# Memory tokens by rows, key/value weights by whole blocks, and two weight blocks at once where an operand's last rows come late

## The chip, the cores and the metric

The kernel runs on one core of one Trainium2 chip. The metric is the time of one execution in device microseconds (us). An execution has one long program for the engines: TensorE (PE, matmuls; PEld is its loading of weights), VectorE (DVE), ScalarE (ACT), GpSimd (POOL) and SyncE (SP), which issues nearly all DMAs.

## What is computed

One layer of a causal decoder, for 1024 tokens of width 1024 in float32. Cut to what matters here:

```python
h = rms_norm(x, norm_mix_pre)
z_pool, z_q, z_rwkv, z_gate = split(h @ w_in)
y_pool = pool_branch(z_pool) @ w_proj_pool       # windows 2, 4, 8, 16 over the tokens
kv     = rms_norm(mem, mem_norm) @ w_mem_kv      # 256 memory tokens, 4 heads of 128
y_mem  = attention(z_q, kv) @ w_proj_mem
y_rwkv = rwkv7(z_rwkv) @ w_proj_rwkv             # 16 heads of 64
gates  = sigmoid(z_gate + gate_b)
merged = gates[0] * y_pool + gates[1] * y_rwkv + gates[2] * y_mem
x = x + rms_norm(merged @ w_o, norm_mix_post)
f = conv_ffn(rms_norm(x, norm_ffn_pre))
x = x + rms_norm(f, norm_ffn_post)
```

## The kernel before

Activations lie transposed: 8 chunks (KC) of 128 channels on the partitions, tokens along the row, in two halves of 512. Each float32 product is made of three matmuls (`mm3`, L164): an operand is split into a high part, cast to the matmul's type (names ending in h or hi), and the rest (l or lo); the three are hi x hi (L167), hi weight x low operand (L168), low weight x hi operand (L169). So each weight chunk has to be split too. `load_w` (L143) loads one block of weights, 1024 rows by 128 columns, in pieces of two chunks (128 KB, tile `wraw`, three buffers for each class c, 0 or 1); `split_w` casts a piece on ACT (`whi`, L128) and subtracts on POOL (`wlo`, L131), or on DVE while `lo_on_dve` is set. `whi` and `wlo` have four buffers a class, one whole block. The classes alternate unless one is asked for, and each has its two PSUM tiles `psg`.

A scheduler sets the order of every engine's instructions ahead of time, from a cost model and priorities; at run time each engine goes through its own row in order and waits on semaphores. `later(a, b)` only sets the order: a is not put ahead of b. Blocks of `w_in` (the products for gates, queries and pooling) are placed into the row of PE as fill between dependent work. They go to DRAM (`d_zg`, `d_zq`, `d_zp`) and are read back later; in the profile they are `psg<-hh` and `psg<-hl`.

The stages that the change touches, in order of time:

- Memory tokens (L744 to L757): one DMA brings `memT` (1 MB, 8 chunks of 128x256) into `mraw`. ACT squares each chunk (`msq`), PE adds the squares over the channels with a matrix of ones (`pmm`, L749), ACT makes 1/rms (`mrs`), DVE scales `mraw` and splits it into `mh`, `ml`.
- Keys and values (L759 on): 8 blocks of `w_kv`, with 256 tokens on the free side; blocks 0 to 3 give K, 4 to 7 give V, which PE also transposes (`pvt`).
- Pooling's sums (`pool_sums`, L779): four loads `tz` of 512 KB from `d_zp`, some six DVE instructions each.
- Attention, four heads, with pooling's products and fill blocks in between; then the projections of attention (`pm`) and pooling (`g`, L886 to L892), each times its gate.
- Merge (`merge`, L911): `yh`, `yl` are the RWKV output, loaded as `yr` and split chunk by chunk (L121, L122; yh0 to yh7). For each half n and each block j: product with `w_prwkv`, times gate, plus `pm`, split into `mgh[j]` and `mgl[n][j]`. `yh`, `yl` of the last chunks lie in memory that pooling's `g` and its operands used before.
- Output product (`wo_gemm`, L1077): 8 blocks of `w_o` on `mgh`, `mgl`, for each half. The blocks of half 1 are started as soon as the merge of half 1 is through.

Of the kernel before, what the change touches and what calls it, by code (L numbers as in the profile page):

```python
# [9 lines left out]
F32 = mybir.dt.float32  # L10
FR = mybir.dt.float32r
AF = mybir.ActivationFunctionType
ALU = mybir.AluOpType
# [4 lines left out]
P = 128  # L18
T = 1024
D = 1024  # L20
KC = D // P
# [23 lines left out]
def trunk_kernel(ctx: ExitStack, tc: tile.TileContext, xT, memT, pvec, w_in, w_kv, w_upd, w_upg,  # L45
                 w_pool, w_ppool, w_pmem, w_prwkv, w_o, w_fup, w_fdn, out):
    nc = tc.nc
    V, A, G, PE, SP = nc.vector, nc.scalar, nc.gpsimd, nc.tensor, nc.sync

    const = ctx.enter_context(tc.tile_pool(name="const", bufs=1))  # L50
    wp = ctx.enter_context(tc.tile_pool(name="wp", bufs=1))
    psg = ctx.enter_context(tc.tile_pool(name="psg", bufs=2, space=PSUM))
# [5 lines left out]
    def dtile(shape, name):  # L58
        return dram.tile(shape, F32, name=name, tag=name)

    d_zp = dtile([4, P, T], "d_zp")
# [12 lines left out]
    def col(name, i):  # L74
        o, w = PV[name]
        return pv[:, o + i:o + i + 1]

    ones = const.tile([P, P], F32, name="ones")
# [16 lines left out]
    for lo in (0, 64):  # L95
        s = slice(lo, lo + 64)
# [3 lines left out]
    for lo in (0, 64):  # L100
        s = slice(lo, lo + 64)
# [18 lines left out]
    def split(src, hi, lo, lo_eng=None):  # L120
        A.copy(hi, src)  # L121
        return (lo_eng or V).tensor_tensor(lo, src, hi.bitcast(F32), op=ALU.subtract)  # L122
# [3 lines left out]
    def split_w(src, hi, lo):  # L126
        if hi_on_act[0]:
            A.copy(hi, src)  # L128
        else:
            G.tensor_scalar(hi, src, 1.0, 0.0, op0=ALU.mult, op1=ALU.add)  # L130
        (V if lo_on_dve[0] else G).tensor_tensor(lo, src, hi.bitcast(F32), op=ALU.subtract)  # L131

    def split_ps(ps, hi, lo):
        split(ps, hi, lo, V)
# [8 lines left out]
    def load_w(ap, nk, kp=2, c=None):  # L143
        if c is None:
            cls[0] ^= 1
            c = cls[0]
        ps = Ws()
        ps.c = c
        for k0 in range(0, nk, kp):
            load_more(ps, ap, k0, min(kp, nk - k0), kp)  # L150
        return ps

    def load_more(ps, ap, k0, n, kp):
        raw = wp.tile([P, kp, P], F32, name="wraw", tag=f"wraw{ps.c}", bufs=3)
        hi = wp.tile([P, kp, P], FR, name="whi", tag=f"whi{ps.c}", bufs=4)
        lo = wp.tile([P, kp, P], FR, name="wlo", tag=f"wlo{ps.c}", bufs=4)
        SP.dma_start(raw[:, :n], ap[:, k0:k0 + n])
        split_w(raw[:, :n], hi[:, :n], lo[:, :n])
        for j in range(n):
            ps.append((hi[:, j], lo[:, j]))  # L160

    last_mm = [None]

    def mm3(ps, w, x, start, stop):  # L164
        wh, wl = w
        xh, xl = x
        first = PE.matmul(ps, wh, xh, start=start, stop=False)  # L167
        PE.matmul(ps, wh, xl, start=False, stop=False)  # L168
        last_mm[0] = PE.matmul(ps, wl, xh, start=False, stop=stop).ins  # L169
        return first  # L170

    def gemm(ws, rhs, width=512, behind=None, ps=None, log=None):

        if ps is None:
            ps = psg.tile([P, 512], F32, name="psg", tag=f"g{getattr(ws, 'c', 0)}")[:, :width]
        n = len(ws)
        for k in range(n):
            m = mm3(ps, ws[k], rhs(k), k == 0, k == n - 1)
            if k == 0 and behind is not None:
                later(m, behind)  # L180
            if log is not None:
                log.append(last_mm[0])
        return ps
# [23 lines left out]
    def later(i, ins):  # L207

        tc.add_manual_dep(i.ins, ins.name, nosync, reason="order")
# [13 lines left out]
    for k in range(KC):  # L223
        tag = ("X01", "X11", "HV", "HV")[k // 2]
# [59 lines left out]

    def hrhs(t0):
        return lambda k: (hh[:, k, t0:t0 + 512], hl[:, k, t0:t0 + 512])

    def in_block(j, evac, c=0, log=None):
        ws = load_w(w_in[j], KC, c=c)
        for t0, _ in HALVES:  # L290
            evac(t0, gemm(ws, hrhs(t0), log=log))
# [448 lines left out]
    vh = kvp.tile([P, 4, 2, P], FR, name="vh")  # L740
    vl = kvp.tile([P, 4, 2, P], FR, name="vl")
    with tc.tile_pool(name="km", bufs=1) as km:
        mraw = km.tile([P, KC, 256], F32, name="mraw")
        SP.dma_start(mraw, memT.rearrange("(k p) t -> p k t", p=P))  # L744
        pmm = psk.tile([P, 512], F32, name="pmm", tag="k")
        for k in range(KC):
            sq = km.tile([P, 256], F32, name="msq", tag="msq", bufs=2)
            A.activation(sq, mraw[:, k], AF.Square)
            PE.matmul(pmm[:, :256], ones, sq, start=k == 0, stop=k == KC - 1)  # L749
        mrs = km.tile([P, 256], F32, name="mrs", tag="msq", bufs=2)  # L750
        rstd(mrs, pmm[:, :256], 0)
        mh = km.tile([P, KC, 256], FR, name="mh")
        ml = km.tile([P, KC, 256], FR, name="ml")
        for k in range(KC):
            V.scalar_tensor_tensor(mraw[:, k], mraw[:, k], col("mem_norm", k), mrs, op0=ALU.mult,
                                   op1=ALU.mult)
            split(mraw[:, k], mh[:, k], ml[:, k], V)  # L757
        lo_on_dve[0] = True
        for j in range(8):  # L759
            ws = load_w(w_kv[j], KC, c=0)  # L760
            ps = gemm(ws, lambda k: (mh[:, k], ml[:, k]), 256)
            if j < 4:
                split_ps(ps, kh[:, j], kl[:, j])
            else:
                vt = km.tile([P, 256], F32, name="vt", tag="msq", bufs=2)
                A.copy(vt, ps)
                pvt = psk.tile([P, 2, P], F32, name="pvt", tag="k")
                for m in range(2):
                    PE.transpose(pvt[:, m], vt[:, m * P:(m + 1) * P], ident)
                split(pvt, vh[:, j - 4], vl[:, j - 4], V)  # L770

        lo_on_dve[0] = False
# [6 lines left out]
    def pool_sums(gi):  # L779
        win = 2 << gi  # L780
        z = pb.tile([P, T], F32, name="tz", tag=f"p{gi}")
        SP.dma_start(z, d_zp[gi])
        two = [pb.tile([P, T], F32, name="ts2", tag=f"l{gi}"),
               pz.tile([P, T], F32, name="ts2", tag="ts") if gi else None]
        cur = z
        w = 1
        n = 0
        while w < win:
            nxt = two[n % 2]
            V.tensor_copy(nxt[:, 0:w], cur[:, 0:w])  # L790
            V.tensor_tensor(nxt[:, w:], cur[:, w:], cur[:, :T - w], op=ALU.add)
            cur = nxt
            w *= 2
            n += 1
        V.tensor_tensor(cur[:, 0:win], cur[:, 0:win], inv[:, 0:win], op=ALU.mult)
        V.tensor_scalar(cur[:, win:], cur[:, win:], 1.0 / win, None, op0=ALU.mult)
        V.tensor_tensor(z, cur, z, op=ALU.subtract)
        zs.append(z)
# [24 lines left out]
    for hd in range(4):  # L823
        for t0, _ in HALVES:
            s = slice(t0, t0 + 512)
# [6 lines left out]
            for u in range(2):  # L832
                ps = psg.tile([P, 2, 256], F32, name="psco", tag="g0")
# [41 lines left out]
    for j in range(8):  # L875
        ws = load_w(w_pmem[j], 4)
        for n, (t0, _) in enumerate(HALVES):
            s = slice(t0, t0 + 512)
            SP.dma_start(pm[j][n], d_zg[16 + j][:, s])
            act(pm[j][n], pm[j][n], AF.Sigmoid)  # L880
            ps = gemm(ws, lambda k: (oh[k][:, s], ol[k][:, s]))
            V.tensor_tensor(pm[j][n], pm[j][n], ps, op=ALU.mult)
    for j in range(8):
        ws = load_w(w_ppool[j], 4)
# [3 lines left out]
        for n, (t0, _) in enumerate(HALVES):  # L888
            s = slice(t0, t0 + 512)
            ps = gemm(ws, lambda k: (ph_[k][:, s], pl_[k][:, s]))  # L890
# [8 lines left out]
    yh, yl = [], []  # L899
# [7 lines left out]
    mgh = [at.tile([P, T], FR, name=f"mgh{k}", tag=f"m{k}") for k in range(KC)]  # L907

    mgl = [[], []]

    def merge(n, js):  # L911
        s = slice(n * 512, n * 512 + 512)
        for j in js:
            ws = load_w(w_prwkv[j], KC)
            gt = yp.tile([P, 512], F32, name="g1", tag="g1", bufs=4)
            SP.dma_start(gt, d_zg[8 + j][:, s])
            act(gt, gt, AF.Sigmoid)
            ps = gemm(ws, lambda k: (yh[k][:, s], yl[k][:, s]))
            V.tensor_tensor(gt, gt, ps, op=ALU.mult)
            V.tensor_tensor(gt, gt, pm[j][n], op=ALU.add)  # L920
            ml_ = pmp.tile([P, 512], FR, name=f"mgl{j}{n}", tag=f"n{2 * j + n}")
            mgl[n].append(ml_)
            split(gt, mgh[j][:, s], ml_, V)
# [148 lines left out]
        rstd(rs, ps, 0)  # L1072
        return rs

    os_, sss = [], []

    def wo_gemm(n, js):  # L1077
        s = slice(n * 512, n * 512 + 512)
        for j in js:
            if j == 0:  # L1080
                o = [(ow if n == 0 else ow1).tile([P, 2, 512], F32, name="o", tag=f"q{4 * n + a}") for a in range(4)]
                os_.append([o[k // 2][:, k % 2] for k in range(KC)])
                sss.append(ow.tile([P, 512], F32, name="ss", tag="ss", bufs=2))
            ws = load_w(w_o[j], KC)
            ps = gemm(ws, lambda k: (mgh[k][:, s], mgl[n][k]))
            V.tensor_copy(os_[n][j], ps)
            sumsq(sss[n], ps, j == 0, V)

# [470 lines left out]
```

## Time and profile before

| what | value |
|---|---|
| time, median of 3 runs | 2114.05 us (2111.07 to 2119.24) |
| profiled execution | 2115.82 us, its span 2114.1 us |
| granted clock of PE, mean | 0.991 |
| busy: PE, DVE, ACT, POOL | 2043.8, 1351.6, 1074.3, 810.1 us |
| DMA | 221.83 MB, mean 105 GB/s |

The profile is of one execution. In its lists an instruction is named by the line of the kernel, the engine, the operation and output<-inputs; `[2.4 <-ACT yh L121]` behind a row says that the engine stood idle for 2.4 us ahead of it and which instruction ended that. SPq is the queue in which SP issues DMAs; the DMA lists end with the median time from issue to landing. Ends of matmuls are modelled, so the text reads PE by the distances between starts: a matmul's row is longer than its distance to the next one.

### The profile page before, as it was taken

Reading aid. Unit: us, or ns where it says so; the run is one execution under the profiler, and the core shown is the slowest. Engines: PE = TensorE matmul, PEld = TensorE weight load, DVE = VectorE, ACT = ScalarE, POOL = GpSimd, SP = SyncE. Lnnn points to the kernel's source line nnn. Section 1 sums busy time; section 2 is a strip of 40 time slices with the busy share of each in tenths; the row PEclk is TensorE's granted clock in tenths of the full one; section 3 lists DMA queues with packets and bytes.
Section 4 is the critical chain, followed back from the end, with each engine's and each line's share of the span. In section 5 each row is a group of like instructions: output and inputs, shape, how many; then the busy total and the mean of one; then the engine's idle time right before and its main releaser. Section 6 shows DMA issues by size and latency. Waiting matters only on the chain.

```text
span 2114.1 us, 34140 instructions
## 1 busy us (share of the span) xinstructions
PE 2043.8 (97%) x12246; PEld 1565.2 (74%) x12246; DVE 1351.6 (64%) x2159; ACT 1074.3 (51%) x2252; POOL 810.1 (38%) x925
## 2 busy tenths in 40 slices
PE   8999999999999999999999999998999999999997
PEld 5777766776768666876777878776778877777886
DVE  6567437654657347733597442668867777776698
ACT  7584347623763367434467244545544444454644
POOL 5521112121122011212021255555678888842341
PEclk9999999999999999999999999999999999999999
DMA  4312111120212021213436343634222222159766
GB/s 153 127 40 78 64 61 58 61 81 22 85 63 90 27 88 43 85 54 115 153 103 221 111 138 102 210 110 152 90 95 75 75 80 80 66 163 280 163 181 155
DMA packets 179193, 221.83 MB, mean 105 GB/s; under 512 B 16720, under 2 KB 131536, under 8 KB 179024
## 3 DMA queue, kind: packets, MB, share of 16 engines
q1 hardware_dynamic: 166096, 204.44, 29.6%
q0 software_dynamic: 11856, 14.16, 4.1%
q8 instruction: 97, 1.59, 0.3%
q10 hardware_dynamic: 1072, 1.05, 0.1%
q14 instruction: 72, 0.59, 0.1%
HBM read 170.30 MB, written 49.28 MB: 104 GB/s over the span
## 4 chain that ended last, share of the span: by engine, by line
PE 44%; DVE 7%; DMA 6%; POOL 6%; ACT 5%; issue 4%; SPq 0%; POOLq 0%; ACTq 0%; DVEq 0%
PE psg L167 9%; PE psg L169 9%; PE psg L168 9%; POOL wt L999 3%; PE psd L168 2%; PE psd L169 2%; PE psd L167 2%; PE psf L169 2%; PE psf L168 2%; PE psf L167 2%; POOL wlo L131 2%; POOL sm L984 1%; DMA a<-in_w_fup 1%; DMA R<-d_f 1%; ACT d L1015 1%
## 5 line engine op out<-in xcount | busy, mean ns | idle before, releaser
L131 POOL TENSOR_TENSOR wlo<-wraw,whi 128x256 fp32r<-128x256 f32 x480 | 413.6, 870 | 987.5 <-ACT whi L128 827.6
L169 PE MATMUL psg<-hh,wlo 128*128 128x512 f32 x928 | 381.0, 411 | 7.4 <-POOL wlo L131 7.1
L167 PE MATMUL psg<-hh,whi 128*128 128x512 f32 x928 | 382.6, 412 | 0.0
L168 PE MATMUL psg<-hl,whi 128*128 128x512 f32 x928 | 377.8, 407 | 0.0
L128 ACT CAST whi<-wraw 128x256 fp32r<-128x256 f32 x496 | 193.7, 404 | 268.1 <-PE psg L168 153.0
L169 PEld LDWEIGHTS psg<-hh,wlo 128*128 128x128 f32 x928 | 174.8, 188 | 54.9 <-POOL wlo L131 14.2
L167 PEld LDWEIGHTS psg<-hh,whi 128*128 128x128 f32 x928 | 175.3, 189 | 41.7 <-issue 2.2
L168 PEld LDWEIGHTS psg<-hl,whi 128*128 128x128 f32 x928 | 175.4, 189 | 41.0 <-issue 2.2
L999 POOL TENSOR_TENSOR wt<-a,wt 128x256 fp32r<-128x256 f32 x136 | 134.3, 1016 | 28.6 <-ACT wt L998 28.6
L167 PE MATMUL psd<-f,u 128*128 128x512 f32 x292 | 115.1, 395 | 6.2 <-ACT f L1297 3.6
L168 PE MATMUL psd<-f,u 128*128 128x512 f32 x292 | 114.9, 394 | 0.9 <-DVE f L1301 0.9
L169 PE MATMUL psd<-f,u 128*128 128x512 f32 x292 | 114.2, 392 | 0.9 <-DVE u L1301 0.9
L999 POOL TENSOR_TENSOR wt<-sm,wt 128x256 fp32r<-128x256 f32 x102 | 106.9, 1068 | 15.7 <-ACT wt L998 15.7
L169 PE MATMUL psf<-h2h,wt 128*128 128x512 f32 x272 | 108.2, 398 | 0.2
L167 PE MATMUL psf<-h2h,wt 128*128 128x512 f32 x272 | 106.7, 392 | 1.3 <-ACT wt L998 1.3
L168 PE MATMUL psf<-h2l,wt 128*128 128x512 f32 x272 | 106.8, 393 | 0.0
L998 ACT CAST wt<-sm 128x256 fp32r<-128x256 f32 x102 | 37.9, 404 | 131.1 <-POOL sm L984 125.7
L1017 DVE SCALAR_TENSOR_TENSOR d<-z,pv,d 128x1023 f32<-128x1023 f32 x68 | 91.7, 1348 | 12.1 <-ACT d L1015 9.5
L169 PE MATMUL psf<-t,wt 128*128 128x512 f32 x204 | 81.2, 398 | 2.2 <-POOL wt L999 2.1
L168 PE MATMUL psf<-t,wt 128*128 128x512 f32 x204 | 80.3, 394 | 0.0
L167 PE MATMUL psf<-t,wt 128*128 128x512 f32 x204 | 80.3, 393 | 0.0
L674 DVE TENSOR_TENSOR HV<-ph,Hd 64x128 f32<-64x128 f32 x112 | 32.3, 288 | 71.5 <-PE ph L630 47.6
(420 smaller groups left out, 4736.6 us busy)
## 6 DMA issues: line engine op xcount, KB each, us to landing
wraw<-in_w_in SPq DMA_DIRECT2D x240, 128.0 KB, 2.4
a<-in_w_fup SPq DMA_DIRECT2D x128, 128.0 KB, 2.4
d_zg<-st SPq DMA_DIRECT2D x48, 256.0 KB, 2.6
wraw<-in_w_fup SPq DMA_DIRECT2D x80, 128.0 KB, 2.4
fw<-in_w_fdn SPq DMA_DIRECT2D x33, 256.0 KB, 4.8
fraw<-d_f SPq DMA_DIRECT2D x33, 256.0 KB, 5.4
wraw<-in_w_prwkv SPq DMA_DIRECT2D x64, 128.0 KB, 2.4
wraw<-in_w_o SPq DMA_DIRECT2D x64, 128.0 KB, 2.4
```

Of the source, the lines that this page charges most:

```text
L128: A.copy(hi, src)
L131: (V if lo_on_dve[0] else G).tensor_tensor(lo, src, hi.bitcast(F32), op=ALU.subtract)
L167: first = PE.matmul(ps, wh, xh, start=start, stop=False)
L168: PE.matmul(ps, wh, xl, start=False, stop=False)
L169: last_mm[0] = PE.matmul(ps, wl, xh, start=False, stop=stop).ins
L674: ready = V.tensor_tensor(HV[q, :, c + 1, e], ph[q], Hd[q], op=ALU.add).ins
L984: eng.tensor_tensor(out_[u], a[u], b[u], op=op)
L998: A.copy(w[0][:, us], src[u])
L999: last_low[0] = G.tensor_tensor(w[1][:, us], src[u], w[0][:, us].bitcast(F32), op=ALU.subtract).ins
L1015: A.activation(d, z, AF.Identity, scale=col("cw2", j), bias=col("cb", j))
L1017: V.scalar_tensor_tensor(d[:, n:], z[:, :T - n], col(cw, j), d[:, n:], op0=ALU.mult, op1=ALU.add)
```

## The change

- The memory tokens are loaded by eight DMAs of one chunk each (128 KB) into two tiles of four chunks with the tag `mraw`; the four `tz` loads are ordered behind the last `pmm` matmul.
- The weights of key/value blocks 2 to 7 are loaded by one DMA of 512 KB each into the same two buffers (`kvr`, tag `mraw`), once the tokens, or an earlier block, have been split out of them. The splits write the same `whi`, `wlo` buffers of class 0 as before.
- `two_gemms` makes two blocks' products at once: the first `late` chunks of the first block, then of the second, then the chunks left of the first and of the second. It is used for the first two blocks of merge, half 0 (late = 6), and of the output product, half 1 (late = 7).

```diff
+    def two_gemms(wss, rhs, late):
+
+        pss_ = [psg.tile([P, 512], F32, name="psg", tag=f"g{ws.c}") for ws in wss]
+        for ks in (range(late), range(late, KC)):
+            for ws, ps in zip(wss, pss_):
+                for k in ks:
+                    mm3(ps, ws[k], rhs(k), k == 0, k == KC - 1)
+        return pss_
...
-        mraw = km.tile([P, KC, 256], F32, name="mraw")
-        SP.dma_start(mraw, memT.rearrange("(k p) t -> p k t", p=P))
+        mraw = [km.tile([P, 4, 256], F32, name="mraw", tag="mraw", bufs=2) for _ in range(2)]
+        mraw = [mraw[k // 4][:, k % 4] for k in range(KC)]
+        for k in range(KC):
+            SP.dma_start(mraw[k], memT[k * P:(k + 1) * P])
...
-            PE.matmul(pmm[:, :256], ones, sq, start=k == 0, stop=k == KC - 1)
+            last_mm[0] = PE.matmul(pmm[:, :256], ones, sq, start=k == 0, stop=k == KC - 1).ins
+        mem_read = last_mm[0]
...
+        def kv_weights(j):
+            raw = km.tile([P, KC, P], F32, name="kvr", tag="mraw", bufs=2)
+            SP.dma_start(raw, w_kv[j])
+            ws = Ws()
+            ws.c = 0
+            for k in range(0, KC, 2):
+                hi, lo = (wp.tile([P, 2, P], FR, name=nm, tag=nm + "0", bufs=4) for nm in ("whi", "wlo"))
+                split_w(raw[:, k:k + 2], hi, lo)
+                ws.extend((hi[:, e], lo[:, e]) for e in range(2))
+            return ws
+
         for j in range(8):
-            ws = load_w(w_kv[j], KC, c=0)
+            ws = kv_weights(j) if j > 1 else load_w(w_kv[j], KC, c=0)
...
-        SP.dma_start(z, d_zp[gi])
+        later(SP.dma_start(z, d_zp[gi]), mem_read)
...
     def merge(n, js):
         s = slice(n * 512, n * 512 + 512)
+        rhs = lambda k: (yh[k][:, s], yl[k][:, s])
+        two = two_gemms([load_w(w_prwkv[j], KC) for j in js[:2]], rhs, 6) if n == 0 else []
         for j in js:
-            ws = load_w(w_prwkv[j], KC)
+            ws = None if two else load_w(w_prwkv[j], KC)
...
-            ps = gemm(ws, lambda k: (yh[k][:, s], yl[k][:, s]))
+            ps = two.pop(0) if two else gemm(ws, rhs)
...
-            ws = load_w(w_o[j], KC)
-            ps = gemm(ws, lambda k: (mgh[k][:, s], mgl[n][k]))
+            rhs = lambda k: (mgh[k][:, s], mgl[n][k])
+            if n == 1 and j == 0:
+                two.extend(two_gemms([load_w(w_o[e], KC) for e in range(2)], rhs, KC - 1))
+            ps = two.pop(0) if two else gemm(load_w(w_o[j], KC), rhs)
```

What this does to the order of instructions. On SP, from the memory tokens on, before:

```order
L744 DMA mraw<-in_memT 128x8x256
L782 DMA tz<-d_zp 128x1024 x4
L318 DMA d_zg<-st 128x512
L157 DMA wraw<-in_w_in 128x256 x4
L157 DMA wraw<-in_w_kv 128x256
L157 DMA wraw<-in_w_in 128x256
L157 DMA wraw<-in_w_kv 128x256 x2
L318 DMA d_zg<-st 128x512
L157 DMA wraw<-in_w_kv 128x256 x4
```

and now (`kvr` are the whole key/value blocks, `uraw` pooling's own weights):

```order
L755 DMA mraw<-in_memT 128x256 x8
L157 DMA wraw<-in_w_in 128x256 x3
L806 DMA tz<-d_zp 128x1024 x4
L774 DMA kvr<-in_w_kv 128x1024
L157 DMA wraw<-in_w_kv 128x256
L774 DMA kvr<-in_w_kv 128x1024
L346 DMA uraw<-in_w_pool 128x128 x2
L327 DMA d_zg<-st 128x512
L157 DMA wraw<-in_w_in 128x256
L346 DMA uraw<-in_w_pool 128x128
L327 DMA d_zg<-st 128x512
L346 DMA uraw<-in_w_pool 128x128
```

The eight rows come first, then three pieces of `w_in` that stood behind `tz`; the key/value loads are fewer, and pieces of `w_in` and stores of `d_zg` stand between them.

On PE, at the memory tokens, before (`pmm<-msq` are the sums of squares, `psg` the fill):

```order
L167 MATMUL psg_10834<-hh_142,whi_10817 128x512
L168 MATMUL psg_10834<-hl_143,whi_10817 128x512
L749 MATMUL pmm_9453<-msq_9454,ones_85 128x256
L749 MATMUL pmm_9453<-msq_9457,ones_85 128x256
L169 MATMUL psg_10834<-hh_142,wlo_10818 128x512
L749 MATMUL pmm_9453<-msq_9460,ones_85 128x256
L749 MATMUL pmm_9453<-msq_9463,ones_85 128x256
L167 MATMUL psg_10834<-hh_142,whi_10817 128x512
L749 MATMUL pmm_9453<-msq_9466,ones_85 128x256
L749 MATMUL pmm_9453<-msq_9469,ones_85 128x256
L168 MATMUL psg_10834<-hl_143,whi_10817 128x512
L749 MATMUL pmm_9453<-msq_9472,ones_85 128x256
```

and now:

```order
L168 MATMUL psg_10587<-hl_143,whi_10554 128x512
L169 MATMUL psg_10587<-hh_142,wlo_10555 128x512
L760 MATMUL pmm_9461<-msq_9462,ones_85 128x256
L760 MATMUL pmm_9461<-msq_9465,ones_85 128x256
L167 MATMUL psg_10587<-hh_142,whi_10554 128x512
L760 MATMUL pmm_9461<-msq_9468,ones_85 128x256
L760 MATMUL pmm_9461<-msq_9471,ones_85 128x256
L168 MATMUL psg_10587<-hl_143,whi_10554 128x512
L760 MATMUL pmm_9461<-msq_9474,ones_85 128x256
L760 MATMUL pmm_9461<-msq_9477,ones_85 128x256
L169 MATMUL psg_10587<-hh_142,wlo_10555 128x512
L760 MATMUL pmm_9461<-msq_9480,ones_85 128x256
```

The sums stand 11 rows, all of them fill matmuls, sooner in PE's row; as before, one fill matmul stands behind each second sum.

On PE, at the first block of merge, before (`psg_12130` is the first block's product, `psg_12187` the second's; yh6, yl6, yh7, yl7 are the last two chunks):

```order
L167 MATMUL psg_12130<-yh5_12075,whi_12116 128x512
L168 MATMUL psg_12130<-yl5_12076,whi_12116 128x512
L169 MATMUL psg_12130<-yh5_12075,wlo_12117 128x512
L167 MATMUL psg_12130<-yh6_12081,whi_12122 128x512
L168 MATMUL psg_12130<-yl6_12082,whi_12122 128x512
L169 MATMUL psg_12130<-yh6_12081,wlo_12123 128x512
L167 MATMUL psg_12130<-yh7_12087,whi_12122 128x512
L167 MATMUL psg_12187<-yh0_12045,whi_12161 128x512
L168 MATMUL psg_12130<-yl7_12088,whi_12122 128x512
```

and now, where the second block begins and where the first is taken up again (`psg_12123` the first block's, `psg_12124` the second's):

```order
L167 MATMUL psg_12123<-yh5_12047,whi_12088 128x512
L168 MATMUL psg_12123<-yl5_12048,whi_12088 128x512
L169 MATMUL psg_12123<-yh5_12047,wlo_12089 128x512
L167 MATMUL psg_12124<-yh0_12017,whi_12100 128x512
L168 MATMUL psg_12124<-yl0_12018,whi_12100 128x512
```

```order
L168 MATMUL psg_12124<-yl5_12048,whi_12112 128x512
L169 MATMUL psg_12124<-yh5_12047,wlo_12113 128x512
L167 MATMUL psg_12123<-yh6_12053,whi_12094 128x512
L168 MATMUL psg_12123<-yl6_12054,whi_12094 128x512
L169 MATMUL psg_12123<-yh6_12053,wlo_12095 128x512
L167 MATMUL psg_12123<-yh7_12059,whi_12094 128x512
L168 MATMUL psg_12123<-yl7_12060,whi_12094 128x512
```

Behind chunk 5 of the first block now stand chunks 0 to 5 of the second, 18 matmuls, and only then yh6. In the output product the same is done with 21 matmuls ahead of chunk 7.

More of the change, by code (lines that the diff above doesn't have):

```diff
@@ L747, in trunk_kernel @@
             sq = km.tile([P, 256], F32, name="msq", tag="msq", bufs=2)
-            A.activation(sq, mraw[:, k], AF.Square)
-            PE.matmul(pmm[:, :256], ones, sq, start=k == 0, stop=k == KC - 1)
+            A.activation(sq, mraw[k], AF.Square)
+            last_mm[0] = PE.matmul(pmm[:, :256], ones, sq, start=k == 0, stop=k == KC - 1).ins
+        mem_read = last_mm[0]
         mrs = km.tile([P, 256], F32, name="mrs", tag="msq", bufs=2)
@@ L754, in trunk_kernel @@
         for k in range(KC):
-            V.scalar_tensor_tensor(mraw[:, k], mraw[:, k], col("mem_norm", k), mrs, op0=ALU.mult,
+            V.scalar_tensor_tensor(mraw[k], mraw[k], col("mem_norm", k), mrs, op0=ALU.mult,
                                    op1=ALU.mult)
-            split(mraw[:, k], mh[:, k], ml[:, k], V)
+            split(mraw[k], mh[:, k], ml[:, k], V)
         lo_on_dve[0] = True
+        def kv_weights(j):
[8 more added lines that the diff above has]
+            return ws
         for j in range(8):
-            ws = load_w(w_kv[j], KC, c=0)
+            ws = kv_weights(j) if j > 1 else load_w(w_kv[j], KC, c=0)
             ps = gemm(ws, lambda k: (mh[:, k], ml[:, k]), 256)
@@ L1073, in norm @@
         return rs
-    os_, sss = [], []
+    os_, sss, two = [], [], []
     def wo_gemm(n, js):
```

## Prediction

> **What bounds the kernel now.** I read the profile's first part for the engine that carries the span, then the waits of TensorE (PE), then the stretches around the four edited places, then their rows in order of time.
>
> ```profile
> PE 2043.8 (97%) x12246; PEld 1565.2 (74%) x12246; DVE 1351.6 (64%) x2159; ACT 1074.3 (51%) x2252; POOL 810.1 (38%) x925
> ```
>
> PE is busy for 97% of the span, so a change that leaves PE's instructions as they are, as this one does, can only win what PE loses in waits or at a low clock. The list of PE's waits (in all, times, longest) has three at the edited places:
>
> ```profile
> PE psg L167 <- ACT yh L121: 2.4, 1, 2.4
> PE pmm L749 <- ACT msq L748: 2.3, 1, 2.3
> PE psg L167 <- ACT mgh L121: 1.8, 1, 1.8
> ```
>
> Each is one single wait. By stretch (PE, PEld, DVE, ACT, POOL busy; granted clock; DMA share; GB/s):
>
> ```profile
> core 0: us, PE busy (x) PEld busy (x) DVE busy (x) ACT busy (x) POOL busy (x), PEclk, DMA share, GB/s
> 1004.95:1007.60 2.65, 0.39 (x2) 0.00 (x0) 0.00 (x0) 0.46 (x2) 0.00 (x0) 1.00 0.99 377
> 1012.40:1056.00 43.60, 40.64 (x258) 34.44 (x257) 24.64 (x56) 21.56 (x58) 4.91 (x6) 1.00 0.36 111
> 1056.00:1131.00 75.00, 71.46 (x406) 57.27 (x405) 71.02 (x131) 49.22 (x131) 17.81 (x20) 1.00 0.43 142
> 1227.40:1231.20 3.80, 3.80 (x11) 2.72 (x10) 1.99 (x3) 0.58 (x2) 2.62 (x3) 0.59 0.31 96
> 1367.00:1371.00 4.00, 3.75 (x10) 2.98 (x11) 0.89 (x2) 0.74 (x2) 1.74 (x3) 0.63 0.72 235
> ```
>
> The first row is the wait for the memory tokens: the DMA engines are full, PE stands. The second is the key/value stage, the third attention, where VectorE (DVE) is busy 71.02 of 75.00 us. The last two follow the waits for yh and mgh: the clock is at 0.59 and 0.63, so the stalls cost more than their waits.
>
> **(a) Memory tokens in rows.** Durations and landing times:
>
> ```profile
> 1003.57 0.45 SPq L782 DMA_DIRECT2D tz<-d_zp  x1
> 1003.78 0.39 PE L169 MATMUL psg<-hh,wlo 128*128 128x512 f32 x1
> 1004.01 0.40 PE L167 MATMUL psg<-hh,whi 128*128 128x512 f32 x1
> 1004.95 0.39 PE L168 MATMUL psg<-hl,whi 128*128 128x512 f32 x1
> 1007.14 0.72 ACT L748 ACTIVATE msq<-mraw 128x256 f32<-128x256 f32 x2 [2.93 <-DMA mraw<-in_memT]
> 1007.61 1.13 PE L749 MATMUL pmm<-msq,ones 128*128 128x256 f32 x4 [2.27 <-ACT msq L748]
> 1012.39 0.47 ACT L199 ACTIVATE mrs<-pmm,eps 128x256 f32<-128x256 f32 x1 [0.79 <-PE pmm L749]
> ...
> wraw<-in_w_kv SPq DMA_DIRECT2D x32, 128.0 KB, 2.4
> g<-d_zg SPq DMA_DIRECT2D x8, 512.0 KB, 4.0
> tz<-d_zp SPq DMA_DIRECT2D x4, 512.0 KB, 7.7
> mraw<-in_memT SPq DMA_DIRECT2D x1, 1024.0 KB, 5.8
> ```
>
> One 512-wide matmul takes 0.23 us of PE (1003.78 to 1004.01). PE's last one before the wait starts at 1004.95, so it could go on at 1005.18; it goes on at 1007.61: 2.43 us lost. The 1 MB load landed at about 1007.1 after 5.8 us, so SP issued it at 1001.3. Issued then, the first 128 KB row lands by 2.4 us at 1003.7, its square ends 0.4 later, so PE can begin at 1004.1 in place of 1007.61; the last row, issued 7 x 0.45 later, lands at 1006.9, before today's whole. But the written order now puts pmm 11 fill matmuls (2.6 us) sooner on PE, so PE comes there at 1002.6 and waits 1.5. What is won is 2.43 - 1.5 = 0.9, not 2.4. The bounds are 2.4 (rows land sooner) and 0 (eight issues and landings cost as much as one big one). Pooling's four loads go on SP behind the rows and three fill loads, some 4 us later; I cost that at nothing, since pooling's sums are wanted in attention only and the stage between, 43.60 us, covers them. What is late next is the normalising of the tokens on DVE, which is as long as before.
>
> On the split into rows the Trainium skill, "DMA: Bandwidth & Descriptors", section Bandwidth, says the opposite: batch transfers to 1 MiB and more. By its fit of 2.0 us + bytes/436 GB/s (section Anatomy of one DMA) I estimate 2.3 us for a row and 4.4 us for the whole; the trace has 2.4 and 5.8. Eight rows one after another at 2.3 would last 18 us, and the term would be a loss of about 8; no row for memT shows whether they overlap, and rival 5 works it out from rows.
>
> **(b) Whole-block weights.** 24 loads of 128 KB become 6 of 512 KB in two buffers; casts and subtractions stay. The rows of the stage:
>
> ```profile
> 1021.79 0.28 PE L169 MATMUL psg<-mh,wlo 128*128 128x256 f32 x1
> 1022.14 0.28 PE L169 MATMUL psg<-mh,wlo 128*128 128x256 f32 x1
> ...
> 1020.77 1.69 DVE L791 TENSOR_TENSOR ts<-tz 128x1023 f32<-128x1023 f32 x1
> 1022.71 0.41 DVE L131 TENSOR_TENSOR wlo<-wraw,whi 128x256 fp32r<-128x256 f32 x1
> ...
> PE psg L167 <- ACT whi L128: 2.7, 4, 1.2
> ...
> SPq L157 <- POOL wlo L131: 41.4, 23, 8.2
> ```
>
> Three 256-wide matmuls start in 0.35 us, so 0.117 each. The window's 258 are 8 x 24 = 192 of these (22.5 us), 8 transposes (some 0.5, an estimate from their width) and 58 fill matmuls (13.4 us): 36.4 of 43.60. So 7.2 us are lost, 2.7 of it in four waits for whi, whose raw chunk had not come; the rest are gaps of 0.1 to 0.5, which the list mostly leaves out. The cause is in SP's row: loads of w_kv stand behind fill loads that wait for POOL's wlo, 41.4 us in 23 waits (this row is of 985 to 1130). In the new order 32 fill matmuls stand in the stage in place of 54; the other 22 (5.1 us) come in attention. A block then gives PE 24 x 0.117 + 4 x 0.23 = 3.7 us, two blocks 7.5. One raw buffer's round is landing 4.0 (as g's 512 KB) + issue 0.45 + ACT's first cast 0.4 + DVE's four subtractions of 0.41, 6.5 us: hidden by 1.0, if DVE comes at once. It does not always: pooling's sums, 1.2 to 1.7 us each, stand in DVE's queue ahead of a wlo; I count 1.69 - 1.0 = 0.7 lost at three places. So: the four waits gone, -2.7; of the other 4.5 a third gone with the fewer loads, -1.5; sums ahead of wlo, +2.1; net 2.1 won. With tz's landing of 7.7 the round is 10.2, 2.7 us late for each of three pairs, and instead of a gain 8 us are lost; with all waits gone it is 5 won. I take 4.0, since a block's load has no other big load beside it, as tz had four.
>
> In attention 22 matmuls more can fill PE's waits, at most 5.1 us; but DVE is busy in 71.02 of 75.00, so no more than 4.0 can go. I take half of 5.1, 2.6; below, -3 if the added fills stand ahead of DVE's producers. (a), (b) and attention: 0.9 + 2.1 + 2.6 = 5.6, range -6 to 11.
>
> **(c) Merge, two blocks to k 5 first.**
>
> ```profile
> 1222.89 0.39 PE L169 MATMUL psg<-yh,wlo 128*128 128x512 f32 x1
> 1223.29 1.20 DVE L892 TENSOR_TENSOR pm<-pm,g 128x512 f32<-128x512 f32 x1
> 1224.57 1.99 ACT L121 CAST yh<-yr 128x1024 fp32r<-128x1024 f32 x2 [2.36 <-DVE pm L892]
> 1225.65 2.36 DVE L122 TENSOR_TENSOR yl<-yr,yh 128x1024 fp32r<-128x1024 f32 x2 [1.17 <-ACT yh L121]
> 1225.67 0.49 PE L167 MATMUL psg<-yh,whi 128*128 128x512 f32 x1 [2.39 <-ACT yh L121]
> 1226.93 0.50 PE L168 MATMUL psg<-yl,whi 128*128 128x512 f32 x1 [0.77 <-DVE yl L122]
> ...
> 1221.37 3.70 POOL L131 TENSOR_TENSOR wlo<-wraw,whi 128x256 fp32r<-128x256 f32 x4 [4.42 <-ACT whi L128]
> ```
>
> yh6 and yh7 are cast when pooling's last add has left their memory (1224.5). PE is free at 1223.12 and starts at 1225.67: 2.55 lost; then 1226.93 in place of 1225.90, 1.03; and 11 matmuls in 3.80 us at clock 0.59, 1.2 more than 11 x 0.23. Some 4.8, with a last gap for yl7 5.1. In the new order 18 matmuls of the second block (4.2 us) stand there. PE then asks for yh6 at 1227.3, yl6 0.23 later, yh7 at 1228.0 and yl7 at 1228.24. The two casts end at 1226.6, the two subtractions at 1228.0: all in time, yl7 by 0.2 only. The second block's weights begin POOL's row at 1221.37 and are used from 1223.12 on: first chunk in time, later ones 0.9 apart against 1.4 of PE's use. I take 4.9; the range is 3 (yl7 or a wlo late) to 5.1.
>
> Here I weigh the clock. The Trainium skill, "TensorE: Matmul & The Clock Gate", Part 1, has the clock halved after an idle window of about 3.4 us. PE's idle here was 2.55 us in one piece and then 1.03, in two pieces over 3.8, and 0.59 followed; the 2.43 us before pmm left 1.00. By that rule a shorter stall need not be followed by slow matmuls, and the rest of the 1.2 here and 1.4 in (d) could be of other origin and stay; the gain would be 2.6 less.
>
> **(d) Output product, two blocks to k 6 first.**
>
> ```profile
> 1363.81 0.39 PE L169 MATMUL psg<-mgh,wlo 128*128 128x512 f32 x1
> 1365.37 0.61 ACT L121 CAST mgh<-g 128x512 fp32r<-128x512 f32 x1
> 1366.02 1.18 DVE L122 TENSOR_TENSOR mgl<-g,mgh 128x512 fp32r<-128x512 f32 x1 [1.38 <-ACT mgh L121]
> 1366.04 0.49 PE L167 MATMUL psg<-mgh,whi 128*128 128x512 f32 x1 [1.84 <-ACT mgh L121]
> 1367.25 0.50 PE L168 MATMUL psg<-mgl,whi 128*128 128x512 f32 x1 [0.72 <-DVE mgl L122]
> 1365.23 3.25 POOL L131 TENSOR_TENSOR wlo<-wraw,whi 128x256 fp32r<-128x256 f32 x4 [1.15 <-ACT whi L128]
> ```
>
> Free at 1364.04, on at 1366.04: 2.00; 1367.25 in place of 1366.27: 0.98; 10 matmuls in 3.75 at clock 0.63: 1.4. Together 4.4. Now 21 matmuls (4.9 us) come first, so mgh7 is asked for at 1368.9 and mgl7 at 1369.2, ready at 1366.0 and 1367.2: hidden by 2 us. The second block's last weights leave POOL at 1368.5 (the row's end) and are asked for after 1368.2, so up to 0.3 can be late. I take 4.3, range 3 to 4.4.
>
> **Sum.** 5.6 + 4.9 + 4.3 = 14.8. The profiled execution took 2115.82 (its span and 1.7 us around it), so 2101.0; the median of the runs, 2114.05, stands 1.8 below it, and 2114.05 - 14.8 gives 2099.3. No engine's work grows, and what follows (c) and (d) runs on weights whose buffers PE frees, so it moves up with PE.
>
> **Rivals.** 0.5% of the time, 10.6 us, is about what a measurement can tell from no change: faster is below 2103.5, slower above 2124.6.
> 1. The gain up to attention's end is lost again: whole-block loads come late, or DVE holds the end of attention. For it: DVE's 71.02 of 75.00, and pooling's sums among the wlo. Against: PE waited there too, and gets 22 fills for it. The terms (c) and (d) stay, 9.2: 2104.9, or 2106.9 if a late load takes 2 us more.
> 2. (c) and (d) give nothing, as the stall comes back for the second block's weights or yl7 and at the low clock. For it: a margin of 0.2; against: 2 us of margin in (d). Then 5.6 remain: 2108.5.
> 3. The slow matmuls at 0.59 and 0.63 stay (the rule weighed in (c) has it so): 2101.9.
> 4. Slower: SP stands in front of the whole-block loads. The new order has fill loads of w_in between the blocks' loads in three places, each of which can wait for POOL's wlo. The longest such wait was 8.2; two blocks give 7.5, a load needs 4.0 + 0.45 + 0.8, so a stand over 2.3 us stalls PE. Three stands of 8.2 cost 3 x 5.9 = 17.7, with slow matmuls after each (1.3, as in (c) and (d)) 21.6, and the 4.7 of the stage and attention do not come: 2099.3 + 26.3 = 2125.6. It decides from three stands of almost 8 us; the mean of the 23 is 1.8.
> 5. The split into eight rows costs eight landings in a row, not one: 8 x 2.4 = 19.2 after 1001.3, so pmm ends near 1021, 8.6 later than now, in place of 0.9 won: 2099.3 + 9.5 = 2108.8. Against it: 377 GB/s in the window up to 1007.60, more than the 55 GB/s of 128 KB in 2.4 us, so loads in flight do overlap.
>
> **How the numbers follow.** Forecast 0.58 (own range 2094 to 2103.5), rival 1 0.18, rival 2 0.08, rival 3 0.08, rival 4 0.05, rival 5 0.03. Faster: the forecast and most of rival 3, with a few hundredths of the others' fast ends, 0.65; slower: rival 4, 0.05; the rest 0.30. For the range, the low end is the sum of the upper bounds, 11 + 5.1 + 4.4 = 20.5, so 2093.5, less 2 for the spread of a median: 2091. The high end takes in rivals 1 to 3 and 5: 2109.
>
> **What would show it.** Right: no wait of PE for yh and mgh above 0.3, granted clock 1.00 in both places, pmm's wait at about 1.5 and its end near 1009, key/value blocks without a wait above 0.7, attention no longer than 79 us. Wrong: kvr named as what PE, ACT or SP wait for, landing above 5; DVE's pooling sums in front of wlo for over 2 us; PE waits for wlo in the second block of (c) or (d); attention stretched by what the stages before it won.

## The result, and the profile after

The changed kernel takes 2100.89 us (median of 5 runs, 2097.17 to 2102.3) against 2115.43 for the kernel before beside it: ratio 0.9924, 95% interval 0.9905 to 0.9943, 16 us less by the ratio. Timed a second time, in another set of runs, it was 0.9926 (0.9904 to 0.9948). Seven executions of all those behind this document took 2194 to 6725 us, and no ratio counts them.

The first part of the profile of the changed kernel, and of the list of PE's waits (in all, times, longest) the rows at the edited places; waits for yh and for mgh are gone from it, and one for `psn` has come (the matmul that adds up `ss`, the squares of the output product's half 1, over the channels for the norm behind it):

```profile
span 2097.7 us, 34129 instructions
PE 2038.1 (97%) x12246; PEld 1564.7 (75%) x12246; DVE 1347.6 (64%) x2159; ACT 1071.2 (51%) x2252; POOL 818.0 (39%) x925
...
PE psn L1094 <- DVE ss L1089: 3.4, 1, 3.4
PE pmm L760 <- ACT msq L759: 1.2, 1, 1.2
PE psg L168 <- DVE mgl L122: 0.2, 1, 0.2
```

The same matmuls run in both kernels, so the two traces can be laid side by side at equal work. I take for each shape the distance of two starts when PE does not wait (0.23 us for a 512-wide matmul, 0.117 for a 256-wide), add these up along PE's rows, and compare the times at which the same sum is reached; the sum of all is 1730 us. What PE gained between two such points, in us, against the one trace of the kernel before (the column "forecast" has the prediction's terms):

| stage (to this sum of work) | forecast | changed kernel | second trace of it |
|---|---|---|---|
| tokens, keys and values (720 to 760) | 3.0 | 5.8 | 4.7 |
| attention and projections (to 900) | 2.6 | 2.5 | 2.7 |
| merge, output product half 0 (to 1040) | 4.9 | 4.7 | 0.8 |
| output product half 1, its start (to 1060) | 4.3 | 4.7 | 4.7 |
| on to the sum of squares, `psn` (to 1100) | 0 | -5.7 | -6.7 |
| the rest (to 1720) | 0 | 4.5 | 4.8 |
| in all | 14.8 | 16.4 | 10.9 |

What a stage shows differs between executions: in kernels in which nothing ahead of merge was changed, single stages ahead of their edits stand up to 1.2 from the kernel before, and the rest -1.2 to 2.9. So stage terms of 2 and more are read from this table, the rest only where it stands far outside that spread, and for the whole the timed ratios are taken.

At the tokens the rows' issues, PE and the squares, then the loads of the stage (KB each, median us to landing), then stretches (columns as in the prediction: the tokens' wait, the key/value stage, the place of the old stall of merge, that of the output product, and two at `psn`):

```profile
1001.02 3.65 SPq L755 DMA_DIRECT2D mraw<-in_memT  x8
1002.23 0.40 PE L169 MATMUL psg<-hh,wlo 128*128 128x512 f32 x1
1003.35 0.72 ACT L759 ACTIVATE msq<-mraw 128x256 f32<-128x256 f32 x2 [1.17 <-DMA mraw<-in_memT]
1003.82 1.13 PE L760 MATMUL pmm<-msq,ones 128*128 128x256 f32 x4 [1.19 <-ACT msq L759]
1008.65 0.47 ACT L199 ACTIVATE mrs<-pmm,eps 128x256 f32<-128x256 f32 x1
...
kvr<-in_w_kv SPq DMA_DIRECT2D x6, 512.0 KB, 3.7
tz<-d_zp SPq DMA_DIRECT2D x4, 512.0 KB, 7.2
mraw<-in_memT SPq DMA_DIRECT2D x8, 128.0 KB, 2.5
...
1008.65:1040.90 32.25, 32.02 (x231) 29.13 (x230) 25.93 (x62) 18.42 (x53) 2.27 (x3) 1.00 0.58 199
1218.00:1222.00 4.00, 4.00 (x19) 3.22 (x18) 1.64 (x4) 0.81 (x2) 4.00 (x6) 1.00 0.35 101
1354.00:1360.00 6.00, 6.00 (x26) 4.55 (x25) 1.45 (x3) 1.81 (x5) 4.17 (x6) 1.00 0.83 264
1397.00:1401.00 4.00, 0.64 (x4) 0.20 (x2) 0.82 (x1) 1.80 (x5) 1.75 (x3) 1.00 0.34 98
1401.00:1405.00 4.00, 4.00 (x9) 2.79 (x10) 0.00 (x0) 1.01 (x3) 2.43 (x4) 0.61 0.45 131
```

The sums of squares begin at 1003.82, not 1007.61, and mrs follows 3.7 us sooner. In the key/value stage PE is busy in 32.02 of 32.25 us. At both old stalls PE is busy throughout, clock 1.00. But at 1397 PE stands for most of 4 us and then runs at 0.61. The rows there:

```profile
1397.23 0.40 PE L169 MATMUL psg<-h2h,wlo 128*128 128x512 f32 x1
1399.18 0.40 ACT L128 CAST whi<-wraw 128x256 fp32r<-128x256 f32 x1 [3.65 <-DMA wraw<-in_w_fup]
1399.49 0.59 ACT L1088 ACTIVATE sq<-psg 128x512 f32<-128x512 f32 x1
1400.12 0.82 DVE L1089 TENSOR_TENSOR ss<-ss,sq 128x512 f32<-128x512 f32 x1 [4.03 <-ACT sq L1088]
1400.99 1.24 PE L1094 MATMUL psn<-ss,ones 128*128 128x512 f32 x2 [3.36 <-DVE ss L1089]
```

The last block's square (`sq`) stands in ACT's row behind a cast of feed-forward weights, and that cast waits 3.65 us for its load; the square's own operand, the product, had been complete since soon after PE's last matmul of it started at 1391.63, and DVE had copied it by 1396.1. The kernel before has the same order, and was only just in time:

```profile
1412.39 0.41 ACT L128 CAST whi<-wraw 128x256 fp32r<-128x256 f32 x1 [3.05 <-DMA wraw<-in_w_fup]
1412.70 0.59 ACT L1062 ACTIVATE sq<-psg 128x512 f32<-128x512 f32 x1
1413.33 0.84 DVE L1063 TENSOR_TENSOR ss<-ss,sq 128x512 f32<-128x512 f32 x1 [3.34 <-ACT sq L1062]
1414.70 1.02 PE L1068 MATMUL psn<-ss,ones 128*128 128x512 f32 x2
```

ss ends at 1414.17, PE asks at 1414.7: 0.5 to spare. So the stall for mgh7 that the change fills would also be time in which the loop of weights (load, cast on ACT, subtraction on POOL, next load) caught up with PE; the experiments test that.

### The profile page after: what moved, and what is told of

It is laid out like the page before. It is cut to its first block, busy times and chain, and to the rows that moved or that the text cites. A ratio compares the mean times of both kernels' runs of the same rounds, so it can differ in the third digit from the quotient of the medians.

```text
span 2097.7 us, 34129 instructions
## 1 busy us (share of the span) xinstructions
PE 2038.1 (97%) x12246; PEld 1564.7 (75%) x12246; DVE 1347.6 (64%) x2159; ACT 1071.2 (51%) x2252; POOL 818.0 (39%) x925
## 4 chain that ended last, share of the span: by engine, by line
PE 26%; DVE 7%; POOL 6%; DMA 6%; issue 4%; ACT 3%; SPq 1%; POOLq 0%; ACTq 0%; DVEq 0%
PE psg L169 5%; PE psg L167 5%; PE psg L168 5%; POOL wt L1025 3%; PE psd L168 2%; PE psd L169 2%; PE psd L167 2%; POOL wlo L131 2%; PE psf L169 1%; POOL sm L1010 1%; PE psf L168 1%; PE psf L167 1%; DMA a<-in_w_fup 1%; ACT d L1041 1%; DMA R<-d_f 1%
## 5 line engine op out<-in xcount | busy, mean ns | idle before, releaser
L131 POOL TENSOR_TENSOR wlo<-wraw,whi 128x256 fp32r<-128x256 f32 x480 | 420.1, 885 | 953.0 <-ACT whi L128 822.0
L128 ACT CAST whi<-wraw 128x256 fp32r<-128x256 f32 x472 | 182.7, 403 | 237.1 <-PE psg L168 114.2
L1025 POOL TENSOR_TENSOR wt<-sm,wt 128x256 fp32r<-128x256 f32 x102 | 106.9, 1068 | 15.7 <-ACT wt L1024 15.7
```

The costliest lines, as they stand in the source:

```text
L1025: last_low[0] = G.tensor_tensor(w[1][:, us], src[u], w[0][:, us].bitcast(F32), op=ALU.subtract).ins
```

## The experiments

Two theories. The prediction's: each place is worth what PE lost there. The loop theory: (c) and (d) put PE ahead of the loop of weights, and what stands in ACT's row behind a cast that waits for its load comes late in turn, so a part returns. For the memory part the question is which of its three pieces is worth what. Time won is (1 - ratio) times the median of the kernel before beside it, 2115 to 2116 us.

| kernel | ratio, 95% interval | us won |
|---|---|---|
| memory part alone | 0.9950, 0.9932 to 0.9967 | 10.6 |
| ... without whole blocks | 0.9971, 0.9957 to 0.9985 | 6.1 |
| ... without pooling's loads behind | 0.9962, 0.9949 to 0.9975 | 8.0 |
| ... tokens in two halves, no rows | 0.9960, 0.9944 to 0.9975 | 8.5 |
| merge's part alone | 0.9989, 0.9977 to 1.0002 | 2.3 |
| output product's part alone | 0.9989, 0.9974 to 1.0004 | 2.3 |
| ... with xts in rows | 0.9981, 0.9966 to 0.9995 | 4.0 |
| xts in rows alone | 0.9994, 0.9982 to 1.0007 | 1.3 |
| changed, without the output product's part | 0.9938, 0.9917 to 0.9958 | 13.1 |
| changed, xts in rows | 0.9931, 0.9909 to 0.9953 | 14.6 |
| changed, squares on DVE | 0.9927, 0.9905 to 0.9949 | 15.4 |
| changed, once more | 0.9926, 0.9904 to 0.9948 | 15.7 |

**The parts one by one.** First the memory part alone: the diff ahead without `two_gemms` and its uses.

> The memory and key/value parts alone (rows, whole blocks, pooling's loads behind), no two_gemms. Chain theory (each place is worth what the two traces show at equal PE work: 1.3 at the tokens, 5.4 in the key/value stage, 1.6 in attention): 8.3 less than before, about 2107.1 against 2115.4. The prediction's terms: 5.6 less, 2109.8. In the profile PE should be 8.3 (or 5.6) ahead of the kernel before when attention is through, and the two stalls of merge and output product should be there as before.

0.9950, 10.6 us. In the trace PE is 7.8 ahead behind attention, and the stalls of merge and output product are back. This sides with the traces' sizes and not with the forecast's 5.6: the interval of time is 7.0 to 14.4. Of what time shows beyond 7.8, the trace has 2.7 at merge, where this kernel edits nothing (see the last section).

Merge's part alone: `two_gemms` and its use in `merge`.

> Merge's first two blocks at once, nothing else. Both theories: the 5.2 lost at yh6 to yl7 with the slow matmuls behind them are won, less a few tenths: PE 4.9 to 5.4 ahead at merge's end, 2110.4. Rival: the casts of yh6 and yh7 hang on pooling's last gate load, which does not move, and the margin of 0.2 at yl7 was luck of the earlier stages' gain; then 3 or less is won.

0.9989, 2.3 us won, with an interval (-0.4 to 4.9) that takes in nothing won at all. At equal work PE wins 5.5 at the place, then loses 1.8 where output product half 0 begins, and 1.7 more by `psn`, where this trace too has a wait, of 1.5, for ss. In the second trace of the changed kernel the first of these places shows why (PE, then ACT, then two stretches):

```profile
1262.95 0.39 PE L169 MATMUL psg<-mgh,wlo 128*128 128x512 f32 x1
1265.41 0.49 PE L167 MATMUL psg<-mgh,whi 128*128 128x512 f32 x1 [2.08 <-ACT mgh L121]
...
1261.67 0.41 ACT L128 CAST whi<-wraw 128x256 fp32r<-128x256 f32 x1 [2.05 <-DMA wraw<-in_w_o]
1262.80 0.63 ACT L199 ACTIVATE g<-g 128x512 f32<-128x512 f32 x1 [0.73 <-DMA g<-d_zg]
1263.45 1.28 ACT L193 ACT_TABLE_LOAD   x1
1264.74 0.62 ACT L121 CAST mgh<-g 128x512 fp32r<-128x512 f32 x1
...
1262.95:1265.60 2.65, 0.57 (x3) 0.19 (x1) 0.21 (x1) 2.62 (x5) 0.00 (x0) 1.00 0.18 55
1265.60:1269.60 4.00, 3.77 (x10) 2.75 (x10) 1.18 (x2) 0.68 (x3) 2.30 (x3) 0.65 0.24 69
```

The cast of mgh7 of half 0 stands behind a gate that waits for its load and a table load, on an ACT that had waited for weights. By starts PE loses 2.2 there. Merge's part alone has the same rows (ACT waits 2.08 for w_o and 0.77 for the gate, PE loses 1.2), and all six traces with merge's part have a loss for mgh there, 0.2 to 2.2; none of the eight without it has. In the kernel before, ACT's casts ahead of this place were held by PE, not by loads:

```profile
1267.74 0.41 ACT L128 CAST whi<-wraw 128x256 fp32r<-128x256 f32 x1 [0.99 <-PE psg L168]
1269.14 0.41 ACT L128 CAST whi<-wraw 128x256 fp32r<-128x256 f32 x1 [0.99 <-PE psg L168]
```

That is the loop theory's reading: with the stall filled, PE is no longer what the loop waits for; the loop is what PE waits for.

Output product's part alone: `two_gemms` and its use in `wo_gemm`.

> The output product's first two blocks at once, nothing else. Chain theory: PE gets 4.2 ahead at the stall's place and gives it all back some 36 us later at psn<-ss, because the last sum of squares hangs on the chain mgl7, xts load of 2 MB, pieces of w_o landing behind it, ACT's casts in front of the squares, which starts from mgl7 and not from PE: 2115 +- 1. The prediction's term: 4.3 less, 2111.1.

0.9989, 2.3 us (-0.8 to 5.5). At equal work 4.7 won at the place and 4.0 lost again by `psn`, where the trace has a wait of 2.8 on DVE's ss: the loop theory. In the rest 2.9 came back; kernels without this part show -1.2 to 2.3 there and the one with xts in rows (below) 0.2, so that is little beyond the spread. By time the part alone is not parted from nothing, nor from the 4.3; only its return by `psn` is shown.

**What holds the square.** In the changed kernel xts (the layer's input x for half 1, which is added behind the norm: 2 MB that are wanted only behind `psn`) goes out at 1354.75 ahead of w_o's pieces; ACT waits for them until 1363.38:

```profile
1354.75 0.39 SPq L1125 DMA_DIRECT2D xts<-in_xT  x1
...
1363.38 0.41 ACT L128 CAST whi<-wraw 128x256 fp32r<-128x256 f32 x1 [5.35 <-DMA wraw<-in_w_o]
```

Here xts comes in rows behind later blocks (`wo_mm` keeps each block's last matmul of half 1):

```diff
-            SP.dma_start(xts, xT[:, s].rearrange("(k p) t -> p k t", p=P))
+            for k in range(KC):
+                later(SP.dma_start(xts[:, k], xT[k * P:(k + 1) * P, s]), wo_mm[2 + 6 * k // KC])
```

> The changed kernel, but xts (2 MB, wanted only after psn<-ss) comes in eight rows of 256 KB, each ordered behind a later block of the output product. Chain theory: the pieces of w_o no longer land behind xts, ACT's squares come 4 to 5 us sooner, the wait at psn<-ss (3.4) and the slow matmuls behind it (1.6) go: 5 less than the changed kernel, about 2096. Rival: the wait at psn has another cause (the loop of three raw buffers, cast, subtraction, load at its own pace): it stays, 2101 as the changed kernel.

```profile
1397.31 0.41 ACT L128 CAST whi<-wraw 128x256 fp32r<-128x256 f32 x1 [3.64 <-DMA wraw<-in_w_fup]
1397.62 0.59 ACT L1088 ACTIVATE sq<-psg 128x512 f32<-128x512 f32 x1
1399.13 1.13 PE L1094 MATMUL psn<-ss,ones 128*128 128x512 f32 x2 [0.93 <-DVE ss L1089]
```

The wait goes from 3.4 to 0.9, and no slow matmuls follow; at equal work 1.2 is lost there and not 5.7. The order (cast, square) and the cast's wait of 3.6 are as before: the whole loop only runs earlier. In time nothing of it is seen, against the 5 us expected: 0.9931 beside 0.9924. The same edit on the kernels without the other parts, with and without the output product's part:

> The kernel before with the output product's two blocks at once and xts in eight rows behind later blocks; nothing else. Chain theory: PE gets 4.5 ahead and keeps most of it past psn<-ss (3 or more of the 4.5; alone it kept 0.7): 2111 to 2112 against 2116. Rival (the squares are late for another reason): 0.7 as without the rows of xts.

> The kernel before with xts in eight rows behind later blocks alone. Chain theory: the chain from the last mgl to the squares gets 4 to 5 shorter, but PE, which loses 4.2 at mgh7, is not held by it: within 1 of before. If xts by itself is worth 3 or more, the chain was the bound before too.

With it the output product's part loses 1.1 by `psn`, not 4.0, and wins 4.0 us in time (1.1 to 7.2); xts in rows alone gives 1.3 (-1.5 to 3.8). So xts ahead of w_o's pieces is one cause of the late loop, shown at its place; that it is worth 2 us in the whole is not resolved.

Then ACT taken out: the squares of blocks 4 to 7 on DVE, with xts in one load.

```diff
+            if n and j > 3:
+                sq = wp.tile([P, 512], F32, name="sq", tag="st", bufs=3)
+                V.tensor_tensor(sq, os_[n][j], os_[n][j], op=ALU.mult)
+                V.tensor_tensor(sss[n], sss[n], sq, op=ALU.add)
```

> The changed kernel with the squares of the output product's blocks 4 to 7, half 1, made on DVE from the copy in place of ACT from PSUM; xts in one load as in the changed kernel. If the last sum is late because ACT's squares stand behind casts that wait for a weight load (chain theory), the wait at psn<-ss goes from 3.4 to below 0.7 and 3 to 5 us with it: 0.990. If it is late for what DVE or the copies do, it stays.

The wait on ss is gone; at equal work 0.5 is lost up to `psn`. That the square was late for its place in ACT's row is shown by this. The time is not better, though (0.9927 beside 0.9926, 0.990 expected). Two of PE's waits in this trace:

```profile
PE psg L167 <- ACT whi L128: 3.6, 3, 3.1
PE psn L1094 <- DVE s L1089: 2.3, 1, 2.3
```

The first is much as in the changed kernel (3.1, longest 2.7). The second is the norm behind, whose list in the changed kernel has no such row; the rest of the program gives -1.4 at equal work where the changed kernel had 4.5. So PE is stopped one wait further on; that this is again the loop was not tried.

**The output product's part in company.**

> The changed kernel without the output product's part. Chain theory: that part wins about 4.7 at its place and gives it back at psn<-ss, so leaving it out costs 0 to 1; 0.992 to 0.993 of before, no psn wait above 0.5, the wait at mgh7 (2 us or less) back. The prediction's term: 4.3 more than the changed kernel, 0.9945.

0.9938 against 0.9926 beside it: the part is worth some 2.5 us, an amount that these intervals do not part from 0 or 5. The trace has a wait of 1.8 at `psn<-ss` even so; the chain is close to PE without this part too, and here the expectation of no wait was wrong.

> The changed kernel once more beside these, on their chip: 0.9924 of before, PE's wait at psn<-ss 2.5 to 4 with slow matmuls behind it.

As expected at `psn`, 3.3; this trace has the wait of 2.1 for mgh of half 0 beside it (above), which was 0.2 in the first.

**The pieces of the memory part.** Without whole blocks (`load_w` for all eight):

> Rows of the tokens and pooling's loads behind, the key/value weights in pieces of 128 KB as before; no two_gemms. If the gain of the stage comes from the whole blocks (theory: pieces of w_kv behind fill loads were what PE waited for), only the 1.3 at the tokens is left of the 8.3 that the memory part won, 0 to 2.5 in all, about 2114. If it comes from the tokens being early and from the fill placed elsewhere, most of the 8 stays, 2108.

With the four loads of `tz` not ordered behind (the call of `later` left out):

> Memory part with rows and whole blocks, but pooling's four loads not ordered behind the sums of squares; no two_gemms. SP then issues them straight behind the rows. The prediction counted the move at nothing: same as the memory part alone (2105.6, PE 7.8 to 8.3 ahead behind attention). Rival: the 2 MB share the DMA engines with the rows or the first whole blocks and 1 to 3 are lost.

With `memT` in two loads of four chunks in place of eight rows:

> The memory part with the tokens in two loads of 512 KB in place of eight rows; whole blocks and pooling's loads behind as changed; no two_gemms. The first half lands by 3.8 to 4.3 after its issue in place of 2.4 for a row, so PE begins the sums 1.3 to 2 later than with rows: 0 to 1.5 less won than the memory part alone (7.8 ahead behind attention, 0.995 of before). Rival: the rows do nothing at all and it is the same.

At equal work, from ahead of the tokens to behind attention and projections: all three pieces 7.8; without whole blocks 2.5; without pooling's loads behind 3.9; without rows 3.4, where at least 6.3 was expected. PE's waits in the key/value stage of these, in this order:

```profile
PE psg L167 <- ACT mh L121: 0.3, 1, 0.3
...
PE psg L167 <- ACT whi L128: 2.4, 4, 0.9
PE psg L167 <- ACT mh L121: 1.0, 1, 1.0
PE psg L169 <- DVE wlo L131: 0.3, 1, 0.3
...
PE psg L167 <- ACT mh L121: 1.6, 1, 1.6
PE psg L167 <- ACT whi L128: 0.3, 1, 0.3
PE pvt L784 <- ACT vt L781: 0.3, 1, 0.3
...
PE psg L167 <- ACT whi L128: 1.0, 1, 1.0
PE psco L169 <- DVE ql L122: 0.4, 1, 0.4
```

Without whole blocks the four waits for whi are back (2.4, before 2.7): pieces of w_kv behind fill loads are what PE waited for, and rows alone win their 1.3 at the sums only to lose 1.0 at mh. With tz ahead the whole blocks land in 4.3, not in 3.5 as in the memory part alone, mh is late by 1.6, and attention waits more (psco for ql 2.4 against 1.3). With halves PE stands 2.3 at the sums, as before the change, and in this trace alone of the four the low clock follows there (last section); the blocks land in 4.2. So the pieces are worth more together than alone, in the traces. In time each missing piece costs 2 to 4.5, and the intervals of the four overlap; without whole blocks 6.1 are won (3.2 to 9.1), more than the 0 to 2.5 expected, though the 4.5 that the whole blocks add is near the trace's 5.3.

## Why the prediction was right, point by point

- **The whole.** 14.8 forecast, 2099.3; measured 2100.89 and 16 by the ratio. The time was met, with terms that were off in opposite directions: the memory part won 10.6 (7.0 to 14.4) and not 5.6, the two blocks at once 2.3 each where 4.9 and 4.3 were forecast, in intervals that reach 4.9 and 5.5. 10.6 + 2.3 + 2.3 = 15.2, so the parts add up within their intervals. That the errors cancelled so closely is luck.
- **(a), met at its place.** PE, last started at 1002.23 and free at 1002.46, waits until 1003.82: 1.36, forecast 1.5; mrs at 1008.65, forecast pmm's end near 1009. A row lands in 2.5, and they overlap: eight issued in 3.65 us, and in this trace the sums never wait for a later one. Rival 5, eight landings in a row, is out. So is the reading of the Trainium skill, "DMA: Bandwidth & Descriptors", section Bandwidth, that loads under 1 MiB should be batched, for this place: halves of 512 KB let PE stand for 2.3. The Trainium skill's rule there is for the rate of a load, and its figures, those of the fit in the prediction too, are of loads issued from GpSimd; these are issued by SP.
- **(a), the step that failed:** "I cost that at nothing", of pooling's loads. In the traces 3.9 of the memory part's 7.8 hang on them (tz ahead: blocks at 4.3, mh late, more waits in attention); by time 2.6, inside the intervals.
- **(b), the term that was mis-sized:** tokens and stage 3.0 forecast, 4.7 to 5.8 measured, of which 1.1 at the tokens. "Sums ahead of wlo, +2.1" did not come: kvr landed in 3.7, and the one wait for wlo in the stage is 0.2. The four waits went as forecast. Of the other 4.5 us of small gaps I let a third go; PE's busy 32.02 of 32.25 leaves little of them. The bounds were loose too: 0, -8 and -3 make -11, not the -6 of the range, and the "5 won" with all waits gone has no working.
- **Attention** won 2.5 against 2.6; rival 1, that it takes back what the stages won, did not come.
- **(c).** The casts were in time, yl7 too in the changed kernel (by 0.35 late in the one with xts in rows: the margin of 0.2 was real). What failed is the sentence on what follows, "runs on weights whose buffers PE frees, so it moves up with PE": the casts of weights wait for loads once PE is ahead, and 0.8 to 1.8 us, 4.4 with the slow clock in the second trace, are lost again where the output product of half 0 begins.
- **(d).** 4.7 at its place as forecast, and the same sentence failed: 5.7 and 6.7 lost again at `psn`. Rival 2 had the return, but of the wrong instruction: not the second block's weights, but a square queued behind a weight cast on ACT. What is late next where a stall goes was asked of PE's operands only, and not of ACT's row.
- **Rival 3, the slow matmuls stay:** out. Where the stalls went the clock is 1.00 (1218 to 1222, 1354 to 1360), where new ones came it is 0.61 and 0.65 behind them. But the 1.2 and 1.4 in (c) and (d) were taken from one trace, as if every execution had them: of eight traces in which the stall at merge stands, six have the slow matmuls behind it, and likewise six of eight at the output product.
- **Rival 4** did not come: PE's one listed wait in the stage of the changed kernel is 0.2.

## What to carry to other kernels

A stall of the busiest engine can also be the time in which the loop that feeds it catches up. Before filling it, look who else was waiting in that time, and in the in-order queues ask what stands behind an instruction that waits for a load: here a square and a cast of the result there became the next stall. Measure the parts alone as well as together: here a sum came out right from one term that was half of what its part won and two that were, as far as the intervals tell, twice too large.

## What the runs showed of the hardware

The low clock comes in steps. Each trace records the stretches of granted clock: a low one has 0.50 and lasts 3.41 us or a multiple of it, but for the last, with which a trace ends. In the kernel before, two start at 1228.05 and 1368.00, 41 steps of 3.413 us apart, and in all fourteen traces the starts stand whole steps apart. Inside such a step matmuls start 0.43 us apart and not 0.23; a stretch that is longer shows the 0.59 to 0.65 of above.

How long PE stood does not tell by itself whether a step follows. With PE's idle time as distances of starts less 0.23, a step followed 2.32 us in one piece ahead of `pmm` (tokens in halves), 2.00 + 0.98 at mgh7 (kernel before) and 1.58 + 0.99 there (memory part alone). None followed 2.43 ahead of `pmm` (kernel before), 2.07 + 0.98 at mgh7 (changed, without the output product's part) or 2.99 at `psn` (output product's part alone). The first and the fifth of these (PE's rows, then the stretch behind the wait):

```profile
1003.61 0.39 PE L167 MATMUL psg<-hh,whi 128*128 128x512 f32 x1
1006.16 2.07 PE L751 MATMUL pmm<-msq,ones 128*128 128x256 f32 x4 [2.16 <-ACT msq L750]
1006.16:1009.57 3.41, 3.41 (x8) 2.78 (x9) 0.00 (x0) 1.97 (x6) 0.51 (x1) 0.50 0.52 180
...
1352.74 0.39 PE L169 MATMUL psg<-mgh,wlo 128*128 128x512 f32 x1
1355.04 0.50 PE L167 MATMUL psg<-mgh,whi 128*128 128x512 f32 x1 [1.91 <-ACT mgh L121]
1356.30:1360.30 4.00, 4.00 (x17) 3.25 (x18) 0.69 (x1) 1.59 (x4) 2.51 (x4) 1.00 0.90 264
```

The idle window of about 3.4 us in the Trainium skill, "TensorE: Matmul & The Clock Gate", Part 1, is longer than the idle time of all six. That it counts where a stall falls on the grid of steps would fit; no run moves a stall alone, so it stays open. At merge of the memory part alone, which edits nothing there, the stall was 1.39 + 1.03 in place of 2.55 + 1.03 and no step followed; PE won 2.7 at the place, and 1.2 of this is the step that did not come.
